# Sparse attention: index queries projected token tile by token tile, the selection of the second query tile begun before the third tile's projection

## The chip, the cores and the metric

The kernel runs on one core of one Trainium2 chip. The metric is the device time of one execution in microseconds (us). TensorE (PE) multiplies, with weight loads shown as an engine of their own (PEld); VectorE (DVE), ScalarE (ACT) and GpSimd (POOL) work on elements; SyncE (SP) starts the transfers between memory and the chip's buffer.

## The reference, cut to what matters

Two decoder layers over 512 tokens of width 1024. Each has a token mixer, a cross attention into 256 memory tokens and a SwiGLU feed-forward network (FFN), and after each of these `x = LayerNorm(alpha * x + y)`. Layer 0 mixes with latent attention, layer 1 with the sparse attention (DSA) that is changed here:

```python
h = x @ w_in            # q 16x64 | k 4x64 | v 4x64 | q_idx 8x64 | k_idx 64 | w_idx 8
...
dots  = einsum('bqhd,bkd->bqhk', q_idx, k_idx) * 64 ** -0.5
score = einsum('bqh,bqhk->bqk', w_idx * 8 ** -0.5, relu(dots))
score = where(causal, score, -inf)
_, sel = top_k(score, 128)           # 128 keys for each query
...                                  # attention over the selected keys, with a bias
```

So for each query of 512 an indexer of eight heads scores all earlier keys; the 128 best keys are kept, and the sixteen heads attend to those alone. Queries of the first token tile (0 to 127) have no more than 128 keys and need no selection.

## The kernel before, in words

Everything is fp32, with each product made of three fast passes: both factors are split into a high and a low part, and `mm3` (L126, L127, L128) adds high x high, high x low and low x high in one PSUM bank. `split` (L102, L104) makes the parts: ACT copies the high part, and DVE (or POOL, if named) subtracts it from the source. `chunk` (L116) loads a piece of weights of up to 128x1024 with SP into `raw`, a ring of three buffers, and splits it into `wh` and `wl`, rings of five. A load waits until the split of the load three places earlier is done with its buffer, and a split until PE is done with the weights five places earlier. PSUM has eight banks, four with the tag "a" and four with "b". `t2` and `t8` are pools of 39 and 9 buffers for intermediate values.

The program is written as one sequence; a scheduler puts it into one fixed order for each engine, and on the chip an engine does its instructions in that order and waits for each one's inputs. So whatever stands behind a waiting instruction on the same engine waits too.

The stages around the change, in the order of the program:

1. *The down-projection of layer 0's FFN* (`out_proj`, n = 0 and then n = 1: the two halves of 512 output columns). For n = 1 it goes over four token tiles of 128 tokens. Behind each tile's products DVE adds the result to x (`residual`, L356), takes statistics (L315), and the tile before is normalised (`Norm.finish`: POOL's L287, DVE's L340, and so on), turned by eight PE transposes (L344) and split for the next stage.
2. *v, index keys and index weights* (loop over token tiles, three chunks of `w_vi`): 24 products of 328 columns for each tile; the keys are copied and transposed (L972), and the four tiles' keys split together.
3. *Index queries and scores*: for each of four pairs of index heads one chunk of `w_qi` is projected for tokens 128 to 511 at once (24 products of 384 columns), split into a stacked form (`stack_q`, DVE's L945 and L946), and scored against the keys for query tiles 1, 2 and 3 (PE's L990 and its neighbour; the relu on ACT, L992; the sum over heads on DVE, L994 for the first head and L996 for the others). Behind the last pair POOL masks the causal triangle of each tile (L999). Tile 1 has 256 keys, tile 2 has 384 and tile 3 has 512.
4. *Selection*: `topk` finds eight maxima of a row (MAX, L1008) and replaces them by a very low number (MATCH_REPLACE, L1009), sixteen such rounds for each of the three tiles, so 48, all on DVE and each dependent on the one before. What was replaced is the selected set, and a last instruction (L1013) makes a mask of it. The rounds are written in between other work: two ahead of each of the two key projections (`w_k`, whose result goes to both halves of the partitions with a subtract on DVE, L1030, and a copy on ACT, L1031), five ahead of each of the eight query projections (`w_q`, low parts of the weights and L953 on POOL), one after each of the next attention items.
5. *Attention*: sixteen items, four query tiles by four groups of heads, each with scores (L1062 to L1064), a softmax (L428, L435, L439, L440), transposes (L1076) with splits (L104, or L107 to L109), the product with v (L1098), and a normalisation (L1100, L1105, L1108, L1109, L1113). The items of tile 0 start inside the query projections.

## Time and profile before

| | |
|---|---|
| median of 3 runs | 1521.48 us (1521.23 to 1521.71) |
| the profiled execution | 1523.14 us, of it 1521.4 us span |
| PE busy | 1490.7 us, 98% of the span |
| DVE busy | 993.9 us, 65% |
| ACT busy | 650.3 us, 43% |
| POOL busy | 305.0 us, 20% |
| granted clock of PE, mean | 0.996 |

A window row of the profile gives the start and end of a stretch, its length, the busy time and the number of instructions of PE, PEld, DVE, ACT and POOL, the granted clock, the busy share of the transfer engines and the rate in GB/s. A timeline row gives start, length, engine, line, operation, output and inputs, and in brackets the idle time before it and what ended that. A group row gives the number of instructions after the x, and behind the bar their busy time in us, the mean of one in ns, and the idle time before them. A row on transfers gives the size of each and the median time from issue to landing in us.

### The profile page before, as it was taken

Reading aid. Unit: us, or ns where it says so; the run is one execution under the profiler, and the core shown is the slowest. Engines: PE = TensorE matmul, PEld = TensorE weight load, DVE = VectorE, ACT = ScalarE, POOL = GpSimd, SP = SyncE. Lnnn points to the kernel's source line nnn. Section 1 sums busy time; section 2 is a strip of 40 time slices with the busy share of each in tenths; the row PEclk is TensorE's granted clock in tenths of the full one; section 3 lists DMA queues with packets and bytes.
Section 4 is the critical chain, followed back from the end, with each engine's and each line's share of the span. In section 5 each row is a group of like instructions: output and inputs, shape, how many; then the busy total and the mean of one; then the engine's idle time right before and its main releaser. Section 6 shows DMA issues by size and latency. Waiting matters only on the chain.

```text
span 1521.4 us, 20233 instructions
## 1 busy us (share of the span) xinstructions
PE 1490.7 (98%) x7642; PEld 1265.9 (83%) x7642; DVE 993.9 (65%) x1739; ACT 650.3 (43%) x1160; POOL 305.0 (20%) x299
## 2 busy tenths in 40 slices
PE   9999999999999999999999989999999999999997
PEld 8788888988898888888898777898889888888886
DVE  7887868554745655654578989675557555666545
ACT  4777753443233333333256588343432433333320
POOL 1322001000032331410024653000002232323002
PEclk9999999999999999999999999999999999999999
DMA  6234424432332233333243146343323233232231
GB/s 216 72 104 114 145 83 131 128 117 70 125 98 92 89 125 98 97 91 104 91 139 104 61 152 224 111 139 97 115 80 125 84 125 97 97 104 78 98 95 56
DMA packets 51143, 166.16 MB, mean 109 GB/s; under 512 B 5284, under 2 KB 11828, under 8 KB 48996
## 3 DMA queue, kind: packets, MB, share of 16 engines
q1 hardware_dynamic: 50468, 163.61, 33.4%
q8 instruction: 60, 0.98, 0.3%
q10 hardware_dynamic: 576, 1.25, 0.2%
q14 instruction: 39, 0.32, 0.1%
HBM read 160.60 MB, written 9.47 MB: 112 GB/s over the span
## 4 chain that ended last, share of the span: by engine, by line
PE 85%; DVE 8%; ACT 2%; issue 2%; DMA 1%; POOL 1%; POOLq 0%; SPq 0%; DVEq 0%; ACTq 0%
PE ps L127 26%; PE ps L126 26%; PE ps L128 26%; DVE t L104 2%; DVE t L1009 2%; DVE m L1008 1%; PE ps L344 1%; ACT t L435 1%; PE ps L1076 1%; DMA t<-scr 1%; ACT t L102 1%; PE ps L660 1%; DVE wl L104 1%; PE ps L786 0%; DVE t L428 0%
## 5 line engine op out<-in xcount | busy, mean ns | idle before, releaser
L126 PE MATMUL ps<-t,wh 128*128 128x512 f32 (+2 forms) x1248 | 451.9, 362 | 6.0 <-DVE t L104 3.4
L127 PE MATMUL ps<-t,wh 128*128 128x512 f32 (+2 forms) x1248 | 450.2, 361 | 1.2 <-DVE t L104 1.2
L128 PE MATMUL ps<-t,wl 128*128 128x512 f32 (+2 forms) x1248 | 450.2, 361 | 0.0
L102 ACT CAST wh<-raw 128x1024 fp32r<-128x1024 f32 (+2 forms) x217 | 226.5, 1044 | 433.5 <-PE ps L127 157.3
L104 DVE TENSOR_TENSOR wl<-raw,wh 128x1024 fp32r<-128x1024 f32 (+2 forms) x196 | 252.6, 1290 | 209.5 <-ACT wh L102 208.5
L126 PE MATMUL ps<-wh,t 128*128 128x512 f32 (+3 forms) x774 | 295.6, 382 | 0.1
L127 PE MATMUL ps<-wl,t 128*128 128x512 f32 (+3 forms) x774 | 293.3, 379 | 0.1
L128 PE MATMUL ps<-wh,t 128*128 128x512 f32 (+3 forms) x774 | 292.9, 378 | 0.0
L126 PEld LDWEIGHTS ps<-t,wh 128*128 128x128 f32 x1248 | 235.5, 189 | 43.2 <-DVE t L104 5.5
L127 PEld LDWEIGHTS ps<-t,wh 128*128 128x128 f32 x1248 | 235.6, 189 | 36.1 <-DVE t L104 1.5
L128 PEld LDWEIGHTS ps<-t,wl 128*128 128x128 f32 x1248 | 235.6, 189 | 35.0
L102 ACT CAST t<-ps 128x512 fp32r<-128x512 f32 (+2 forms) x249 | 122.6, 526 | 129.6 <-PE ps L344 86.5
L126 PEld LDWEIGHTS ps<-wh,t 128*128 128x128 f32 x774 | 146.6, 189 | 25.7 <-ACT t L435 0.4
L128 PEld LDWEIGHTS ps<-wh,t 128*128 128x128 f32 x774 | 146.4, 189 | 25.8
L127 PEld LDWEIGHTS ps<-wl,t 128*128 128x128 f32 x774 | 146.5, 189 | 25.6 <-DVE wl L104 0.5
L287 POOL TENSOR_TENSOR sm<-sm,mhalf 128x1 f32<-128x1 f32 x32 | 30.2, 942 | 682.6 <-DVE sm L285 682.6
L104 DVE TENSOR_TENSOR t<-ps,t 128x512 fp32r<-128x512 f32 (+2 forms) x249 | 143.4, 607 | 19.9 <-ACT t L102 17.6
L102 ACT CAST wh<-t 128x1024 fp32r<-128x1024 f32 x56 | 58.9, 1053 | 141.8 <-PE ps L127 123.6
L104 DVE TENSOR_TENSOR wl<-t,wh 128x1024 fp32r<-128x1024 f32 x56 | 71.3, 1273 | 65.2 <-ACT wh L102 63.2
L889 DVE TENSOR_TENSOR t<-ps,t 128x512 f32<-128x512 f32 x44 | 30.4, 692 | 120.1 <-PE ps L128 120.1
L104 DVE TENSOR_TENSOR t<-t,t 128x512 fp32r<-128x512 f32 (+2 forms) x113 | 84.5, 751 | 27.9 <-ACT t L102 25.7
L102 ACT CAST t<-t 128x512 fp32r<-128x512 f32 (+2 forms) x113 | 64.6, 575 | 56.8 <-POOL t L823 33.6
(179 smaller groups left out, 1645.1 us busy)
## 6 DMA issues: line engine op xcount, KB each, us to landing
raw<-in_ffn_in_dram SPq DMA_DIRECT2D x88, 512.0 KB, 3.5
t<-in_ffn_dg_dram SPq DMA_DIRECT2D x16, 1024.0 KB, 5.1
raw<-in_xa_k_dram SPq DMA_DIRECT2D x16, 512.0 KB, 3.6
raw<-in_xa_v_dram SPq DMA_DIRECT2D x16, 512.0 KB, 3.6
raw<-in_xa_q_dram SPq DMA_DIRECT2D x16, 512.0 KB, 4.3
raw<-in_xa_o_dram SPq DMA_DIRECT2D x16, 512.0 KB, 3.5
raw<-in_ffn_dl_dram SPq DMA_DIRECT2D x12, 512.0 KB, 3.5
scr<-vscr SPq DMA_DIRECT2D x16, 319.5 KB, 4.3
```

What stands on the lines that cost most here:

```text
L102: nc.scalar.copy(h, src)
L104: low[0] = (eng or nc.vector).tensor_tensor(l, src, h.bitcast(F32), op=ALU.subtract)
L126: nc.tensor.matmul(ps, st[0], mv[0], start=start, stop=False, skip_group_check=more)
L127: nc.tensor.matmul(ps, st[0], mv[1], start=False, stop=False, skip_group_check=more)
L128: nc.tensor.matmul(ps, st[1], mv[0], start=False, stop=stop, skip_group_check=more)
L287: nc.gpsimd.tensor_tensor(b, a, mhalf, op=ALU.pow)
L344: nc.tensor.transpose(pt[:, k], x_of(tt)[:, 512 * n + P * k:512 * n + P * k + P], ident)
L435: nc.scalar.activation(Sx, src, AF.Exp, bias=nb, scale=scale, accum_out=self.sm[:, i:i + 1])
L660: nc.tensor.transpose(pt[:, P * qt:P * qt + P], Ss[qt][:, P * kb:P * kb + P], ident)
L889: nc.vector.tensor_tensor(sg, pu, sg, op=ALU.mult)
L1008: nc.vector.max(out=m8, in_=acc[:, :n])
L1009: nc.vector.match_replace(out=acc[:, :n], in_to_replace=m8, in_values=acc[:, :n], imm_value=-3e38)
```

## The change

Four things are done in other ways. First, `w_qi` is laid out by input rows, and its four pieces are loaded and split by `load_wqi`, which the down-projection of layer 0's FFN calls behind its own last weight loads (`mid`). The eight pairs of split pieces (512 columns each) stay in `t2` buffers until the projections are done. Second, index queries are projected for one token tile at a time, with tokens on the output's partitions (`index_q`: 24 products of 512 columns for each of tiles 1, 2 and 3), then copied by ACT, turned back by four PE transposes (`index_turn`) and stacked. Third, scores are made by tile and by half of the heads (`index_scores`, HA the first four and HB the last four), and keys are transposed and split for each tile. Fourth, the order: tile 1's scores are complete before tile 3's index query projection, and selection rounds begin there, four of them ahead of tile 3's turn, two ahead of the first key projection, four more behind tile 3's first scores, two ahead of the second key projection, and then five ahead of each query projection as before.

```diff
...
-    def out_proj(src, w, kc, norm, first, pins=()):
+    def out_proj(src, w, kc, norm, first, pins=(), mid=None):
...
             ws = [weights(n, c) for c in range(kc)] if n else None
+            if n and mid:
+                mid()
...
-    def ffn(i, XT, norm_of, between=None):
+    def ffn(i, XT, norm_of, between=None, mid=None):
...
-        out_proj(lambda k: H[k], lambda n, c: A["ffn_dl"][i, n, c], len(H) // 2, norm, False)
+        out_proj(lambda k: H[k], lambda n, c: A["ffn_dl"][i, n, c], len(H) // 2, norm, False, mid=mid)
...
-    norm = ffn(0, norm.XT, lambda: Norm(load_ln(0, 2), spill=True), general_bias())
+    wqi = []
+
+    def load_wqi():
+        for c in range(4):
+            raw = wp.tile([P, 1024], F32, tag="raw", name=nm("raw"), bufs=3)
+            nc.sync.dma_start(raw, A["w_qi"][c])
+            for i in range(2):
+                wqi.append((t2(FR), t2(FR)))
+                split(*wqi[-1], raw[:, 512 * i:512 * i + 512])
+
+    norm = ffn(0, norm.XT, lambda: Norm(load_ln(0, 2), spill=True), general_bias(), load_wqi)
     r = nc.values_load(flag[0:1, 0:1], engines=(mybir.EngineType.SP,), min_val=0, max_val=1)
     XT = norm.XT
 
...
 
     wvs = [chunk(A["w_vi"][:, NV * k0:NV * k1], (P, k1 - k0, NV)) for k0, k1 in ((0, 3), (3, 6), (6, 8))]
     VD = t8(FR, (P, 4, 4, P))
-    pk = bank("b")
     wi = cp.tile([P, NT, 8], F32, name="wi")
-    for tt in range(NT):
+    KIA, KIB = t2(FR), t2(FR)
+    masks = [None] + [t2() for _ in range(1, NT)]
+
+    def dsa_v(tt):
         pv = bank("a")
-        ts_ = slice(P * tt, P * tt + P)
+        ts_ = ts_of(tt)
         for k in range(NK):
             xh, xl = k_of(XT, k)
             w = wvs[k // 3]
             mm3(pv[:, 0:NV], (xh[:, ts_], xl[:, ts_]), (w[0][:, k % 3], w[1][:, k % 3]), k == 0, k == NK - 1)
+        ki = t2(F32, (P, 2, 64))
+        nc.scalar.copy(ki, pv[:, 264:NV].unsqueeze(1).broadcast_to((P, 2, 64)))
+        nc.vector.tensor_scalar(wi[:, tt], pv[:, 256:264], 8.0 ** -0.5, None, op0=ALU.mult)
+        pk = bank("b", (P, P))
+        nc.tensor.transpose(pk, ki.rearrange("p a b -> p (a b)"), ident)
+        split(KIA[:, ts_], KIB[:, ts_], pk)
         pv4 = pv[:, 0:256].rearrange("p (g d) -> p g d", g=4)
         split(VD[:, tt, :, 0:64], VD[:, tt, :, 64:128], pv4)
-        nc.vector.tensor_scalar(wi[:, tt], pv[:, 256:264], 8.0 ** -0.5, None, op0=ALU.mult)
-        ki = t2(F32, (P, 2, 64))
-        nc.scalar.copy(ki, pv[:, 264:NV].unsqueeze(1).broadcast_to((P, 2, 64)))
-        nc.tensor.transpose(pk[:, ts_], ki.rearrange("p a b -> p (a b)"), ident)
-
-    KIA, KIB = t2(FR), t2(FR)
-    split(KIA, KIB, pk)
-    masks = [None] + [t2() for _ in range(1, NT)]
-    for j in range(4):
-        pq = bank("a")
-        proj(pq, chunk(A["w_qi"][j], (P, NK, P)), XT, (P, S))
+
+    def index_q(qt):
+        ps = bank("a")
+        ts_ = ts_of(qt)
+        for k in range(NK):
+            xh, xl = k_of(XT, k)
+            mm3(ps, (xh[:, ts_], xl[:, ts_]), wqi[k], k == 0, k == NK - 1)
+        qf = t2()
+        nc.scalar.copy(qf, ps)
+        return qf
+
+    def index_turn(qf):
+        pt = bank("a")
+        for j in range(4):
+            nc.tensor.transpose(pt[:, P * j:P * j + P], qf[:, P * j:P * j + P], ident)
         qi = (t2(FR), t2(FR))
-        stack_q(pq[:, P:], qi[0][:, P:], qi[1][:, P:])
-        for qt in range(1, NT):
-            n = P * (qt + 1)
-            ts_ = slice(P * qt, P * qt + P)
-            acc = masks[qt]
-            for e in range(2):
-                h = 2 * j + e
-                ps = bank("b")
-                nc.tensor.matmul(ps[:, :n], qi[e][:, ts_], KIA[:, :n], start=True, stop=False)
-                nc.tensor.matmul(ps[:, :n], qi[e][:, ts_], KIB[:, :n], start=False, stop=True)
-                rl = t2()
-                nc.scalar.activation(rl[:, :n], ps[:, :n], AF.Relu, scale=0.125)
-                if h == 0:
-                    nc.vector.tensor_scalar(acc[:, :n], rl[:, :n], wi[:, qt, 0:1], None, op0=ALU.mult)
-                else:
-                    nc.vector.scalar_tensor_tensor(acc[:, :n], rl[:, :n], wi[:, qt, h:h + 1], acc[:, :n],
-                                                   op0=ALU.mult, op1=ALU.add)
-            if j == 3:
-                nc.gpsimd.affine_select(out=acc[:, n - P:n], in_=acc[:, n - P:n], pattern=[[-1, P]],
-                                        compare_op=ALU.is_ge, fill=-1e30, base=0, channel_multiplier=1)
+        stack_q(pt, qi[0], qi[1])
+        return qi
+
+    def index_scores(qt, qi, heads):
+        n = P * (qt + 1)
+        acc = masks[qt]
+        for h in heads:
+            js = slice(P * (h // 2), P * (h // 2) + P)
+            ps = bank("b")
+            nc.tensor.matmul(ps[:, :n], qi[h % 2][:, js], KIA[:, :n], start=True, stop=False)
+            nc.tensor.matmul(ps[:, :n], qi[h % 2][:, js], KIB[:, :n], start=False, stop=True)
+            rl = t2()
+            nc.scalar.activation(rl[:, :n], ps[:, :n], AF.Relu, scale=0.125)
+            if h == 0:
+                nc.vector.tensor_scalar(acc[:, :n], rl[:, :n], wi[:, qt, 0:1], None, op0=ALU.mult)
+            else:
+                nc.vector.scalar_tensor_tensor(acc[:, :n], rl[:, :n], wi[:, qt, h:h + 1], acc[:, :n],
+                                               op0=ALU.mult, op1=ALU.add)
+        if heads[-1] == 7:
+            nc.gpsimd.affine_select(out=acc[:, n - P:n], in_=acc[:, n - P:n], pattern=[[-1, P]],
+                                    compare_op=ALU.is_ge, fill=-1e30, base=0, channel_multiplier=1)
+
     MK = t8()
 
     def topk(qt, its):
...
 
     todo = [(qt, [i]) for qt in range(1, NT) for i in range(TOPK // 8)]
     NTK, NTI = 5, 1
+
+    def rounds(n):
+        for _ in range(min(n, len(todo))):
+            topk(*todo.pop(0))
+
     KA, KB = [], []
-    for j in range(2):
-        for _ in range(2):
-            topk(*todo.pop(0))
+
+    def k_proj(j):
+        rounds(2)
         (pk,) = proj_tiles([chunk(A["w_k"][j], (P, NK, P), nc.gpsimd)], XT, False)
         kt_ = t8()
         for e in range(2):
...
             nc.scalar.copy(kb[64 - 64 * e:128 - 64 * e], kb[64 * e:64 * e + 64].bitcast(F32))
             KA.append(ka)
             KB.append(kb)
+
+    HA, HB = range(0, 4), range(4, 8)
+    dsa_v(0)
+    dsa_v(1)
+    f1 = index_q(1)
+    dsa_v(2)
+    i1 = index_turn(f1)
+    f2 = index_q(2)
+    index_scores(1, i1, HA)
+    dsa_v(3)
+    index_scores(1, i1, HB)
+    i2 = index_turn(f2)
+    f3 = index_q(3)
+    index_scores(2, i2, HA)
+    rounds(4)
+    i3 = index_turn(f3)
+    k_proj(0)
+    index_scores(2, i2, HB)
+    index_scores(3, i3, HA)
+    rounds(4)
+    k_proj(1)
+    index_scores(3, i3, HB)
+
     def dsa_bias(qt, g):
         n = P * (qt + 1)
         c0 = 127 + 384 - 128 * qt
...
-        for _ in range(min(NTK, len(todo))):
-            topk(*todo.pop(0))
+        rounds(NTK)
...
-        for _ in range(NTI):
-            if todo:
-                topk(*todo.pop(0))
+        rounds(NTI)
...
-    f["w_qi"] = _fm(w[:, 1536:2048])
+    f["w_qi"] = _tm(w[:, 1536:2048], 2, 512)[0]
```

On DVE at the end of layer 0's down-projection (`wl` from `ffn_dl` are raw_10118 and raw_10124, raw_10324 is the first piece of `w_vi`; L356 is the residual add), before:

```order
L104 TENSOR_TENSOR wl_10121<-raw_10118,wh_10120 128x1024
L104 TENSOR_TENSOR t_1386_9996<-t_1382_9988,t_1385_9995 128x512
L104 TENSOR_TENSOR wl_10127<-raw_10124,wh_10126 128x1024
L104 TENSOR_TENSOR wl_10327<-raw_10324,wh_10326 128x984
L356 TENSOR_TENSOR t_658_2508<-t_658_2508,ps_10006 128x512
L356 TENSOR_TENSOR t_658_2508<-t_658_2508,ps_10007 128x512
L315 BN_STATS sm_10101<-t_658_2508 128x6
```

and now, with raw_10130 to raw_10160 the four pieces of `w_qi` and raw_10364 the first of `w_vi`:

```order
L104 TENSOR_TENSOR wl_10121<-raw_10118,wh_10120 128x1024
L104 TENSOR_TENSOR t_1420_10133<-raw_10130,t_1419_10132 128x512
L104 TENSOR_TENSOR t_1422_10137<-raw_10130,t_1421_10136 128x512
L104 TENSOR_TENSOR t_1425_10143<-raw_10140,t_1424_10142 128x512
L104 TENSOR_TENSOR wl_10127<-raw_10124,wh_10126 128x1024
L104 TENSOR_TENSOR t_1427_10147<-raw_10140,t_1426_10146 128x512
L104 TENSOR_TENSOR t_1430_10153<-raw_10150,t_1429_10152 128x512
L104 TENSOR_TENSOR t_1432_10157<-raw_10150,t_1431_10156 128x512
L104 TENSOR_TENSOR t_1435_10163<-raw_10160,t_1434_10162 128x512
L104 TENSOR_TENSOR t_1437_10167<-raw_10160,t_1436_10166 128x512
L104 TENSOR_TENSOR wl_10367<-raw_10364,wh_10366 128x984
L356 TENSOR_TENSOR t_658_2508<-t_658_2508,ps_10006 128x512
```

Between the last split of the down-projection's weights, the first split of `w_vi` and the first residual add there are now eight subtracts of `w_qi`.

On POOL, from the normalisation at the end of that FFN (L287) to the causal masks (L999, now L1024), before, where the five splits are those of two pieces of `w_k` and three of `w_q`:

```order
L287 TENSOR_TENSOR sm_10220<-sm_10218,mhalf 128x1
L287 TENSOR_TENSOR sm_10266<-sm_10264,mhalf 128x1
L287 TENSOR_TENSOR sm_10293<-sm_10291,mhalf 128x1
L104 TENSOR_TENSOR wl_10787<-raw_10784,wh_10786 128x1024
L104 TENSOR_TENSOR wl_10833<-raw_10830,wh_10832 128x1024
L104 TENSOR_TENSOR wl_10891<-raw_10888,wh_10890 128x1024
L104 TENSOR_TENSOR wl_10945<-raw_10942,wh_10944 128x1024
L104 TENSOR_TENSOR wl_11000<-raw_10997,wh_10999 128x1024
L999 AFFINE_SELECT t_1463_10473<-t_1463_10473 128x128
L999 AFFINE_SELECT t_1464_10474<-t_1464_10474 128x128
L999 AFFINE_SELECT t_1465_10475<-t_1465_10475 128x128
L104 TENSOR_TENSOR wl_11056<-raw_11053,wh_11055 128x1024
```

and now:

```order
L287 TENSOR_TENSOR sm_10260<-sm_10258,mhalf 128x1
L287 TENSOR_TENSOR sm_10306<-sm_10304,mhalf 128x1
L104 TENSOR_TENSOR wl_10736<-raw_10733,wh_10735 128x1024
L104 TENSOR_TENSOR wl_10845<-raw_10842,wh_10844 128x1024
L287 TENSOR_TENSOR sm_10333<-sm_10331,mhalf 128x1
L104 TENSOR_TENSOR wl_10931<-raw_10928,wh_10930 128x1024
L104 TENSOR_TENSOR wl_10985<-raw_10982,wh_10984 128x1024
L104 TENSOR_TENSOR wl_11039<-raw_11036,wh_11038 128x1024
L1024 AFFINE_SELECT t_1474_10386<-t_1474_10386 128x128
L104 TENSOR_TENSOR wl_11096<-raw_11093,wh_11095 128x1024
L1024 AFFINE_SELECT t_1475_10387<-t_1475_10387 128x128
L104 TENSOR_TENSOR wl_11176<-raw_11173,wh_11175 128x1024
```

Both `w_k` splits moved ahead of the last tile's L287, and the three masks, which stood together, are each behind a `w_q` split.

On DVE around the first selection round (L1008 and L1009, now L1034 and L1035; L996 and now L1019 and L1021 are the sums over heads; t_1463 and t_1474 are the scores of tile 1), before:

```order
L996 SCALAR_TENSOR_TENSOR t_1463_10473<-t_1527_10735,wi,t_1463_10473 128x256
L996 SCALAR_TENSOR_TENSOR t_1463_10473<-t_1529_10741,wi,t_1463_10473 128x256
L996 SCALAR_TENSOR_TENSOR t_1464_10474<-t_1531_10750,wi,t_1464_10474 128x384
L1008 MAX m_1539_10778<-t_1463_10473 128x8
L996 SCALAR_TENSOR_TENSOR t_1464_10474<-t_1533_10756,wi,t_1464_10474 128x384
L996 SCALAR_TENSOR_TENSOR t_1465_10475<-t_1535_10765,wi,t_1465_10475 128x512
L1009 MATCH_REPLACE t_1463_10473<-m_1539_10778,t_1463_10473 128x256
L996 SCALAR_TENSOR_TENSOR t_1465_10475<-t_1537_10771,wi,t_1465_10475 128x512
L1008 MAX m_1540_10781<-t_1463_10473 128x8
```

and now:

```order
L1021 SCALAR_TENSOR_TENSOR t_1474_10386<-t_1512_10636,wi,t_1474_10386 128x256
L957 TENSOR_TENSOR t_1514_10647<-ps_10642,t_1514_10647 64x512
L958 TENSOR_TENSOR t_1515_10648<-ps_10642,t_1515_10648 64x512
L1034 MAX m_1526_10704<-t_1474_10386 128x8
L1035 MATCH_REPLACE t_1474_10386<-m_1526_10704,t_1474_10386 128x256
L1034 MAX m_1527_10707<-t_1474_10386 128x8
L1035 MATCH_REPLACE t_1474_10386<-m_1527_10707,t_1474_10386 128x256
L1034 MAX m_1528_10710<-t_1474_10386 128x8
L1035 MATCH_REPLACE t_1474_10386<-m_1528_10710,t_1474_10386 128x256
L1034 MAX m_1529_10713<-t_1474_10386 128x8
L1019 TENSOR_SCALAR t_1475_10387<-t_1519_10683,wi 128x384
L1035 MATCH_REPLACE t_1474_10386<-m_1529_10713,t_1474_10386 128x256
```

Before, the first round stands between the last three sums of tiles 2 and 3; now it stands behind tile 1's last sum and tile 2's stacking (L957, L958), and all of the sums of tiles 2 and 3 come behind it, in between rounds.

## The prediction

> **What bounds the kernel now.** I read the page first. It says TensorE (PE), nearly everywhere:
>
> ```profile
> span 1521.4 us, 20233 instructions
> PE 1490.7 (98%) x7642; PEld 1265.9 (83%) x7642; DVE 993.9 (65%) x1739; ACT 650.3 (43%) x1160; POOL 305.0 (20%) x299
> ```
>
> PE is idle for 30.7 us of the span. So I asked next where those are, with the windows around the changed stage (columns: busy us and instructions of PE, PEld, DVE, ACT, POOL; granted clock; DMA share; GB/s):
>
> ```profile
> 750.00:760.00 10.00, 9.99 (x48) 8.03 (x47) 9.73 (x18) 1.18 (x2) 1.39 (x2) 1.00 0.30 105
> 850.00:860.00 10.00, 8.80 (x46) 7.10 (x46) 9.74 (x32) 7.30 (x18) 3.14 (x4) 1.00 0.01 2
> 860.00:870.00 10.00, 7.91 (x37) 6.34 (x38) 9.68 (x26) 4.77 (x11) 5.26 (x8) 1.00 0.01 2
> 870.00:880.00 10.00, 8.14 (x46) 6.83 (x45) 9.66 (x35) 5.08 (x14) 8.24 (x10) 1.00 0.49 157
> 880.00:890.00 10.00, 7.15 (x48) 5.95 (x48) 8.08 (x27) 8.00 (x28) 2.44 (x6) 0.92 0.00 1
> 890.00:900.00 10.00, 10.00 (x54) 9.44 (x53) 7.74 (x30) 7.45 (x23) 6.40 (x9) 0.74 0.54 185
> 900.00:910.00 10.00, 9.60 (x55) 7.52 (x55) 8.86 (x30) 9.41 (x23) 6.52 (x14) 1.00 0.61 210
> 889.00:890.00 1.00, 0.60 (x3) 0.61 (x4) 1.00 (x3) 0.67 (x2) 1.00 (x3) 0.50 0.00 0
> ```
>
> From 850 to 890 PE works 32.0 us of 40: 8.0 us idle, while VectorE (DVE) is 97% busy until 880. There DVE sets the time. Second finding: a granted clock of 0.50 at 889, a mean of 0.92 and 0.74 in the two slices around it. 0.92 means 1.6 us at half, 0.74 means 5.2 us: 6.8 us at half speed, some 3.4 us of work lost. The timeline names the waits in brackets:
>
> ```profile
> 860.43 0.50 PE L126 MATMUL ps<-t,wh 128*128 128x512 f32 x1 [1.29 <-ACT t L952]
> 869.00 0.44 PE L1108 MATMUL ps<-ident,t 128*128 128x128 f32 x2 [1.65 <-POOL t L440]
> 878.36 0.35 PE L1063 MATMUL ps<-t,t 128*128 128x256 f32 x1 [1.59 <-DVE sm L428]
> 886.63 0.63 PE L1076 MATMUL ps<-ident,t 128*128 128x128 f32 x4 [1.89 <-DVE t L1105]
> 888.16 0.62 PE L1098 MATMUL ps<-t,t 128*128 128x512 f32 x1 [0.34 <-ACT t L109]
> 889.40 0.69 PE L1108 MATMUL ps<-ident,t 128*128 128x128 f32 x2 [0.61 <-POOL t L440]
> 813.29 0.43 DVE L1008 MAX8 m<-t 128x8 f32<-128x256 f32 x1 [0.19 <-POOL t L999]
> 813.64 1.26 DVE L996 SCALAR_TENSOR_TENSOR t<-t,wi,t 128x384 f32<-128x384 f32 x2
> 814.82 0.08 DVE L1009 MATCH_VALUE_LOAD t<-m,t 128x8 f32 x1
> 885.64 0.84 DVE L1105 TENSOR_TENSOR t<-ps,t 64x256 f32<-64x256 f32 x2
> ```
>
> The last three waits before 889.4 add up to 2.84 us and lie among transposes; behind them PE starts at half clock. DVE's queue runs from the first selection round (813.29) to the operation that releases PE (885.64): 72.35 us. When this queue ends decides when PE runs free again.
>
> **The change, part by part.**
>
> *Tail of layer 0's FFN.* Four w_qi loads and eight splits now stand ahead of the first w_vi split, and that ahead of the first residual add, on DVE and in the raw ring of three.
>
> ```profile
> 737.29 1.05 ACT L102 CAST wh<-raw 128x1024 fp32r<-128x1024 f32 x1 [4.10 <-issue]
> 738.38 1.23 DVE L104 TENSOR_TENSOR wl<-raw,wh 128x1024 fp32r<-128x1024 f32 x1 [3.84 <-ACT wh L102]
> 743.78 1.18 DVE L104 TENSOR_TENSOR wl<-raw,wh 128x984 fp32r<-128x984 f32 x1 [4.18 <-ACT wh L102]
> 746.09 1.37 DVE L356 TENSOR_TENSOR t<-t,ps 128x512 f32<-128x512 f32 x2 [1.12 <-PE ps L128]
> L104 DVE TENSOR_TENSOR t<-raw,t 128x512 fp32r<-128x512 f32 x4 | 2.6, 684 | 0.0
> raw<-in_ffn_dl_dram SPq DMA_DIRECT2D x6, 512.0 KB, 3.5
> raw<-in_w_q_dram SPq DMA_DIRECT2D x2, 512.0 KB, 4.8
> ```
>
> Of the eight subtracts (0.68 each), three fit into the idle 3.84 us ahead of the last down-projection split, which ended at 739.6 and now ends near 740.4. That frees the slot for the third w_qi load (740.4); the fourth (740.8) and the first w_vi load (741.1, once the second load's last subtract is done) go right behind on SP's queue. A load alone takes 3.5 us, two close together 4.8; three I estimate at a little over 5: w_vi is there at 746.3, its cast (1.05) and subtract (1.18) end at 748.6. The residual add, at 746.09 now, waits for that: **+2.5**. Bounds: w_vi in 3.5 us gives 746.9, +0.8; the three one after another at 3.5 each give 753.2, +7.1. I take 2.5, by the nearest row (4.8). It is not hidden: those adds free PE's banks for the token projections, and DVE's share of 0.97 from 750 to 760 shows no slack to catch up in.
>
> *PE's own work.*
>
> ```profile
> 783.08 0.31 PE L126 MATMUL ps<-wh,t 128*128 128x328 f32 x1
> 783.52 0.34 PE L126 MATMUL ps<-t,wh 128*128 128x384 f32 x1
> ...
> 784.57 0.33 PE L126 MATMUL ps<-t,wh 128*128 128x384 f32 x1
> 829.37 0.39 PE L126 MATMUL ps<-t,wh 128*128 128x512 f32 x1
> 830.05 0.39 PE L126 MATMUL ps<-t,wh 128*128 128x512 f32 x1
> 249.18 0.87 PE ps L344 x8
> ```
>
> Three products lie between neighbouring L126 rows (784.57 is the second after 783.52); the last row is the chain's, eight transposes in 0.87. Index projections: 96 of 384 columns at 0.175 (1.05 for six) = 16.8; now 72 of 512 at 0.227 (0.68 for three) = 16.3. Twelve transposes more at 0.109 = 1.3. Net **+0.8** on PE, hidden while DVE bounds.
>
> *First selection round.* Now the four v projections end at 783.5. The first third of the fourth ends five k-steps of 0.44 earlier, 781.3; in the new order two index projections (10.9), one turn (0.4), four scores of 256 columns (eight products, about 1.0 by 0.147 for 328 columns) and the 2.5 above come first: 796.1. That third's weight slots are what the first w_q chunk waits for, and in POOL's order three w_q splits now stand ahead of tile 1's causal select:
>
> ```profile
> 829.60 2.41 POOL L104 TENSOR_TENSOR wl<-raw,wh 128x1024 fp32r<-128x1024 f32 x1 [2.12 <-ACT wh L102]
> L999 POOL TENSOR_SCALAR_AFFINE_SELECT t<-t 128x128 f32<-128x128 f32 x3 | 1.7, 572 | 3.2 <-DVE t L996 3.2
> ```
>
> Cast 1.05, three splits of 2.41 with starts between them, select 0.57: the first round starts near **805.3** instead of 813.29. Without these splits ahead it would be 2.5 earlier, since the last scores of tile 1 end by 801.
>
> Two more edits I cost at nothing. On POOL two w_k splits now stand ahead of the last tile's L287, the power that its normalisation needs; their cover is the time until that tile's statistics are there, by my walk some 1.2 us more than the splits need. If it is gone, one split (2.41) lands on tile 3's projections and on the first round. On SP's queue the four w_qi loads leave the place behind w_vi, so that w_k and w_q come sooner; PE waits for neither there, so nothing is gained, and a delay of one load (3.5) would be hidden behind the two index projections.
>
> *DVE's queue from there.* It loses the three sums behind 813.29 (1.26 + 0.75) and gains sixteen sums of tiles 2 and 3, a stacking pair for tile 3, and the last mask, which stood behind 885.64:
>
> ```profile
> L996 DVE SCALAR_TENSOR_TENSOR t<-t,wi,t 128x512 f32<-128x512 f32 x7 | 5.2, 748 | 0.3
> L996 DVE SCALAR_TENSOR_TENSOR t<-t,wi,t 128x384 f32<-128x384 f32 x7 | 4.3, 617 | 0.3
> L1030 DVE TENSOR_TENSOR t<-ps,t 64x512 fp32r<-64x512 f32 x4 | 2.8, 689 | 0.1
> L1013 DVE TENSOR_SCALAR t<-t 128x512 fp32r<-128x512 f32 x1 | 0.4, 427 | 0.0
> ```
>
> The sums are L996's, each tile's first one (a plain multiply) taken at the same price; the pair is priced by L1030, a subtract of the same shape, and the mask is L1013.
>
> 72.35 − 2.0 + 8 × 0.617 + 8 × 0.748 + 2 × 0.689 + 0.43 = 83.1. Against that, sums between a round's MAX and its MATCH_REPLACE overlap both: 0.43 + 1.26 took 1.53 (813.29 to 814.82), 0.16 saved. In DVE's order 16 fewer neighbours belong to one chain of rounds: 16 × 0.16 = 2.6 saved (half that if only one edge overlaps). 80.5 us: the queue ends at 885.8, **+0.2**, between −2.3 (tail +0.8, select 0.8 sooner) and +4.8 (tail +7.1). So the early start is eaten by the longer queue.
>
> PE arrives at the queue's end later: 2.5 + 0.8, and I estimate 1.8 for a new stall at 818 to 821. There tile 3's scores need a bank whose relu stands on ACT behind a key copy, which waits for a DVE subtract behind the rounds. A wait of this kind is there now:
>
> ```profile
> 819.54 0.62 ACT L1031 CAST t<-t 64x512 fp32r<-64x512 f32 x1 [1.63 <-DVE t L1030]
> ```
>
> These 5.1 us replace idle time: of the 8.0 us some 3 stay, and the free run starts where the queue lets it, 0.2 later.
>
> *The clock.* The waits of 1.89, 0.34 and 0.61 us shrink, PE being later, and the emptied stretch before 889 with them. I take **−2.5** of the 3.4 us, and 0 and −3.4 as bounds: DVE and ACT stay busy to 0.89 and 0.94 at 900 to 910, so some PE time regained there will be lost to waits.
>
> The Trainium skill, "TensorE: Matmul & The Clock Gate", section "What's actually happening", has a free-running window of 3413 ns and half rate after an idle one, and "Part 4: PE-mode transpose" adds that transposes do not count as busy in the same way. Read by gaps alone (its section "Why this matters for your kernels" allows gaps up to some 3 us) the 1.89 us here would have cost no clock; the trace disagrees, unless the transposes among the waits count as idle. By that stricter reading the clock term would be 0 for me as well, the time of the first rival.
>
> Sum: +0.2 − 2.5 = −2.3. The profiled execution took 1523.14 us, 1.7 above its span and 1.7 above the median of 1521.48; it would become 1520.8, the median **1519.2**.
>
> **Rivals.** *1. The clock falls anyway* (chance 0.22). The new stall at 818, or the 3 us of waits that remain after 855, empty a window as the old one did. For it: summed waits of only 2.8 us did it once. Against: the same waits at 860 to 879, each 1.3 to 1.65 us, did not. Time: 1521.48 + 0.2 = 1521.7.
>
> *2. The tail is cheap* (0.20). w_vi lands in 3.5 us, first round at 803.6, queue end 884.1 (−1.5), the whole clock loss gone (−3.4): 1516.6; with the select ahead of one split less, 2.4 less, 1514.2. For it: DMA share is only 0.30 at 750 to 760. Against: three loads start within 0.7 us.
>
> *3. Slower* (0.17). The three loads land one behind the other at 3.5 us each, the residual adds come 7.1 later and everything behind them 4.6 later than forecast: first round 809.9, queue end 890.4, +4.8, and PE meets the same waits with the same half clock. Time 1521.48 + 4.8 = 1526.3. It decides from 3.0 us on, that is when w_vi lands more than 8 us after its issue at the same clock loss. For it: nothing on SP's queue orders w_vi ahead. Against: 4.8 us for two.
>
> **How the numbers follow.** The forecast has 0.38, 0.03 is left over. Its own range is 1517 to 1521.2: clock −3.4 to −1, queue −1 to +0.7. About 0.2% (3.0 us) is what a measurement of this kernel can tell from no change: 1518.4 to 1524.5 is "same". Faster: rival 2 with 0.19 and some 0.4 of the forecast, 0.36 in all. Slower: rival 3 with 0.15, some of rival 1 with a longer tail, 0.22. Same: 0.42. For eight in ten I go from 1514.8, nearly rival 2's far end, to 1525.8, most of rival 3.
>
> **What would show it.** The residual add at 748.6 (below 747: rival 2; above 750: rival 3). The first MAX at 805.3. The three POOL splits ahead of tile 1's select. DVE busy 0.95 or more from there to about 886. PE idle of 3 us instead of 8 from 850 to 890, and no slice with clock 0.50 between 880 and 900; a half clock elsewhere says rival 1. The forecast is wrong if the free run starts more than 2 us from 889.6, or if PE stalls in a place not named here, above all between 796 and 821, where the new order puts ACT copies and splits behind each other.

## The result: 1533.7 us, slower by 0.8%

| | before | after |
|---|---|---|
| median | 1521.6 us (1521.2 to 1521.9, 4 runs) | 1533.7 us (1533.0 to 1535.9, 4 runs) |
| ratio, 95% interval | | 1.0082 (1.0065 to 1.0099) |
| profiled execution, span | 1523.1, 1521.4 us | 1534.0, 1532.2 us |

I had forecast 1519.2 and a range up to 1525.8. One execution in all that follows, of kernel 9 below, took 8403.9 us and is left out of its median. Profiled executions of kernels that are alike up to the changed stage reach it at times up to 2.8 us apart, so I measure the stage by itself: from SP's first load for the down-projection (`ffn_dl`) to its fifth load for layer 1's cross-attention values (`xa_v`). Timelines of before and, below, of after:

```profile
698.79 24.63 SPq L116 DMA_DIRECT2D raw<-in_ffn_dl_dram  x6
1038.59 12.50 SPq L116 DMA_DIRECT2D raw<-in_xa_v_dram  x4
```

```profile
698.22 24.63 SPq L116 DMA_DIRECT2D raw<-in_ffn_dl_dram  x6
1049.39 5.76 SPq L116 DMA_DIRECT2D raw<-in_xa_v_dram  x2
```

339.8 us became 351.2, +11.4: all of the loss is here. The windows of after (columns as in the prediction) show where PE lost it:

```profile
740.00:750.00 10.00, 9.37 (x42) 7.42 (x41) 6.75 (x11) 4.17 (x6) 0.00 (x0) 1.00 0.72 232
770.00:780.00 10.00, 6.98 (x32) 6.66 (x33) 8.05 (x11) 1.81 (x4) 4.50 (x3) 0.66 0.47 158
810.00:820.00 10.00, 8.51 (x42) 6.80 (x41) 9.53 (x25) 3.74 (x8) 0.29 (x1) 1.00 0.18 54
820.00:830.00 10.00, 7.29 (x33) 5.57 (x32) 9.60 (x27) 7.38 (x15) 2.87 (x2) 1.00 0.15 52
890.00:900.00 10.00, 8.46 (x51) 7.63 (x51) 5.48 (x29) 7.91 (x29) 1.93 (x4) 0.83 0.08 27
900.00:910.00 10.00, 9.45 (x53) 8.60 (x54) 7.98 (x30) 8.02 (x25) 8.00 (x12) 0.83 0.49 182
```

From 700 to 950 PE is idle for 16.8 us; before it was 9.5. And there are now two stretches at half clock, one at 770 to 780 (0.66: 6.8 us at half, 3.4 lost) and the old one (0.83 twice, 3.4 lost). 7.2 of idle time, 3.4 of clock and the 0.8 forecast for added products and transposes make up the 11.4. The timeline of after names two pairs of rows that I had not looked for:

```profile
768.45 5.26 POOL L104 TENSOR_TENSOR wl<-raw,wh 128x1024 fp32r<-128x1024 f32 x2
768.65 5.61 DVE L340 SCALAR_TENSOR_TENSOR t<-t,sm,t 128x512 f32<-128x512 f32 x2
771.56 1.12 PE L344 MATMUL ps<-ident,t 128*128 128x128 f32 x4 [2.14 <-DVE t L340]
774.41 1.09 PE L344 MATMUL ps<-ident,t 128*128 128x128 f32 x4 [1.46 <-DVE t L340]
805.41 5.58 DVE L1021 SCALAR_TENSOR_TENSOR t<-t,wi,t 128x256 f32<-128x256 f32 x4
812.46 0.43 DVE L1034 MAX8 m<-t 128x8 f32<-128x256 f32 x1
827.82 0.50 PE L1014 MATMUL ps<-t,t 128*128 128x512 f32 x1 [2.37 <-ACT t L1017]
```

The same work before, tile 2's L340 and the group of the sums of 256 columns:

```profile
767.39 1.41 DVE L340 SCALAR_TENSOR_TENSOR t<-t,sm,t 128x512 f32<-128x512 f32 x2
L996 DVE SCALAR_TENSOR_TENSOR t<-t,wi,t 128x256 f32<-128x256 f32 x7 | 3.4, 485 | 2.1 <-ACT t L992 2.1
```

Tile 2's two L340, 1.41 us together for any other tile, took 5.61 while POOL made the low parts of w_k. Tile 1's last four sums, 0.485 us each before, took 5.58 while POOL made those of w_q (three of them from 802.23). PE waited 2.14 us, fell to half clock at 771.4 and waited another 1.46; the first round came at 812.46, only 0.8 sooner than before. I read this as DVE being held by POOL. That reading, and what the rest is worth, had to be tested.

### The profile page after: what moved, and what is told of

Its sections match the earlier page's. It is cut to its first block, busy times and chain, and to the rows that moved or that the text cites. A ratio compares the mean times of both kernels' runs of the same rounds, so it can differ in the third digit from the quotient of the medians.

```text
span 1532.2 us, 20237 instructions
## 1 busy us (share of the span) xinstructions
PE 1494.5 (98%) x7630; PEld 1266.0 (83%) x7630; DVE 1002.1 (65%) x1744; ACT 651.5 (43%) x1168; POOL 304.6 (20%) x299
## 4 chain that ended last, share of the span: by engine, by line
PE 84%; DVE 10%; ACT 3%; issue 2%; DMA 1%; POOL 0%; POOLq 0%; SPq 0%; DVEq 0%; ACTq 0%
PE ps L127 26%; PE ps L126 26%; PE ps L128 26%; DVE t L1035 2%; DVE t L104 2%; DVE m L1034 1%; ACT t L437 1%; PE ps L344 1%; DMA t<-scr 1%; ACT t L102 1%; DVE t L1021 1%; PE ps L1130 1%; DVE wl L104 1%; PE ps L662 1%; ACT wh L102 1%
## 5 line engine op out<-in xcount | busy, mean ns | idle before, releaser
L126 PE MATMUL ps<-t,wh 128*128 128x512 f32 (+1 forms) x1216 | 441.3, 363 | 5.9 <-DVE t L104 3.4
L127 PE MATMUL ps<-t,wh 128*128 128x512 f32 (+1 forms) x1216 | 439.5, 362 | 1.2 <-DVE t L104 1.2
L128 PE MATMUL ps<-t,wl 128*128 128x512 f32 (+1 forms) x1216 | 439.4, 361 | 0.0
L102 ACT CAST wh<-raw 128x1024 fp32r<-128x1024 f32 (+2 forms) x213 | 222.2, 1044 | 424.7 <-PE ps L127 157.3
L104 DVE TENSOR_TENSOR wl<-raw,wh 128x1024 fp32r<-128x1024 f32 (+2 forms) x192 | 247.5, 1290 | 200.1 <-ACT wh L102 198.9
L126 PEld LDWEIGHTS ps<-t,wh 128*128 128x128 f32 x1216 | 229.5, 189 | 43.3 <-DVE t L104 5.5
L127 PEld LDWEIGHTS ps<-t,wh 128*128 128x128 f32 x1216 | 229.6, 189 | 35.7 <-DVE t L104 1.5
L128 PEld LDWEIGHTS ps<-t,wl 128*128 128x128 f32 x1216 | 229.5, 189 | 34.9
L287 POOL TENSOR_TENSOR sm<-sm,mhalf 128x1 f32<-128x1 f32 x32 | 30.1, 942 | 683.4 <-DVE sm L285 683.4
```

The lines of the kernel that those rows point to most:

```text
L102: nc.scalar.copy(h, src)
L104: low[0] = (eng or nc.vector).tensor_tensor(l, src, h.bitcast(F32), op=ALU.subtract)
L126: nc.tensor.matmul(ps, st[0], mv[0], start=start, stop=False, skip_group_check=more)
L127: nc.tensor.matmul(ps, st[0], mv[1], start=False, stop=False, skip_group_check=more)
L128: nc.tensor.matmul(ps, st[1], mv[0], start=False, stop=stop, skip_group_check=more)
L287: nc.gpsimd.tensor_tensor(b, a, mhalf, op=ALU.pow)
```

## The experiments

All comparisons are with the kernel before on the same chip, whose median in these sets was 1520.8 to 1521.6. The stage is that of the one profiled execution. The last column splits it further: PE's idle time in it, and what was lost to the clock (half of the time at a granted clock of 0.50).

| kernel | median | ratio (95%) | stage | idle / clock |
|---|---|---|---|---|
| before | | 1 | 339.8 | 9.7 / 3.4 |
| the change | 1533.7 | 1.0082 (1.0065 to 1.0099) | 351.2 | 16.9 / 6.8 |
| 1. w_k low parts on DVE | 1528.0 | 1.0048 (1.0031 to 1.0064) | 345.5 | 13.8 / 3.4 |
| 2. w_q low parts behind the select | 1532.6 | 1.0075 (1.0058 to 1.0091) | 351.5 | 16.3 / 8.5 |
| 3. 1 and 2 | 1526.3 | 1.0031 (1.0019 to 1.0044) | 343.6 | 11.0 / 5.1 |
| 4. the change, short POOL splits | 1526.6 | 1.0031 (1.0018 to 1.0043) | 346.9 | 14.4 / 5.1 |
| 5. the change, key copies on POOL | 1530.6 | 1.0063 (1.0045 to 1.0080) | 348.4 | 17.1 / 3.4 |
| 6. 3 and key copies on POOL | 1524.8 | 1.0031 (1.0018 to 1.0043) | 342.6 | 12.9 / 1.7 |
| 7. 3 without the early rounds | 1526.3 | 1.0027 (1.0017 to 1.0037) | 344.0 | 11.9 / 5.1 |
| 8. 6 and short splits ("all mends") | 1520.7 | 0.9995 (0.9986 to 1.0005) | 339.8 | 11.4 / 0 |
| 9. before, short splits | 1519.2 | 0.9979 (0.9969 to 0.9989) | 337.6 | 8.8 / 1.7 |
| 10. 8, tile 1's scores ahead of q of tile 2 | 1521.1 | 0.9995 (0.9985 to 1.0005) | 341.9 | 10.5 / 1.7 |
| 11. 8, tile 1's scores ahead of the fourth v | 1520.9 | 0.9997 (0.9987 to 1.0006) | 339.3 | 10.4 / 0 |
| 12. 8, w_qi loads behind w_vi | 1520.3 | 0.9992 (0.9983 to 1.0002) | 338.9 | 10.0 / 1.7 |
| 13. 9, half of the rounds | 1516.3 | 0.9966 (0.9952 to 0.9980) | 333.3 | 5.9 / 0 |
| 14. 8, half of the rounds | 1515.3 | 0.9967 (0.9953 to 0.9981) | 336.0 | 8.2 / 0 |

The clock differs between executions of one kernel too: of kernel 6's eight, two had a mean granted clock of 0.993 and took 1528.7 and 1528.8 us, six had 0.995 to 0.999 and took 1523.8 to 1525.7. So a clock term of 1.7 or 3.4 us in one profiled execution is not yet a property of the kernel.

### Does POOL hold DVE? (1 to 4)

Kernel 1 puts the low parts of w_k on DVE, behind the last split of the normalisation (`done`):

```diff
     XT = norm.XT
+    done = low[0]
-        (pk,) = proj_tiles([chunk(A["w_k"][j], (P, NK, P), nc.gpsimd)], XT, False)
+        (pk,) = proj_tiles([chunk(A["w_k"][j], (P, NK, P), None, (None, done))], XT, False)
```

> The two low-part subtracts of w_k are on DVE, behind the last split of the FFN's last normalisation, and POOL has none until w_q. Theory A (a DVE instruction with two operands in SBUF stands still while POOL's subtract runs): the second L340 of tile 2, 2.83 us with the change, is back at 0.72 to 0.75, as is the first; PE's waits of 2.14 and 1.46 us at 771 to 775 go, and with them the half clock of 770 to 780 (mean 0.66, 3.4 us lost): 5 to 7 us less, 1527 to 1529. Tile 1's last sums still meet POOL's w_q splits and stay near 1.4 us each. Theory B (the new order itself is late: w_vi behind w_qi, and the stalls at 811 to 828; the long L340 only fills time in which PE would wait anyway): first MAX still after 811, time 1532 to 1534. Theory C (the length of L340 is a wait for POOL's power, L287, counted as busy): L340 stays near 2.8 us.

Groups of lines from 740 to 910, kernel 1:

```profile
L340 DVE SCALAR_TENSOR_TENSOR t<-t,sm,t 128x512 f32<-128x512 f32 x8 | 5.6, 744 | 0.0
L1022 DVE SCALAR_TENSOR_TENSOR t<-t,wi,t 128x256 f32<-128x256 f32 x7 | 6.7, 960 | 1.0 <-ACT t L1018 0.5
```

All eight L340 have a mean of 744 ns again (with the change 1270). The clock is 1.00 up to 820, and the stage is 5.7 us shorter, the time 1528.0, as A had it. L287 stayed on POOL, so C falls. Tile 1's sums still have a mean of 960: nothing was done for them.

Kernel 2 puts the w_q low parts of the first three chunks behind tile 1's select (`sel[1]` is its instruction):

```diff
-            nc.gpsimd.affine_select(...)
+            sel[qt] = nc.gpsimd.affine_select(...)
...
-        (pq,) = proj_tiles([chunk(A["w_q"][j], (P, NK, P), nc.gpsimd)], XT, False)
+        (pq,) = proj_tiles([chunk(A["w_q"][j], (P, NK, P), nc.gpsimd, (None, sel[1] if j < 3 else None))], XT, False)
```

> The low parts of the first three w_q chunks stand on POOL behind tile 1's causal select, the w_k ones stay where the change has them. Theory A: tile 1's last four sums take 0.48 to 0.5 us each in place of 1.4 (4 in 1.95 instead of 5.58), the first MAX is near 808.8 instead of 812.5, PE's wait of 1.29 us at 811.8 goes; tile 2's sums may meet the splits in turn, up to 2.4 us for each that does: 1530 to 1533. The tile 2 L340 stays at 2.8 and the half clock of 770 to 780 stays. Theory B: the first MAX sooner by the POOL queue alone (one select, under 1 us), 1533 to 1534.

Groups of kernel 2:

```profile
L340 DVE SCALAR_TENSOR_TENSOR t<-t,sm,t 128x512 f32<-128x512 f32 x8 | 9.8, 1270 | 0.0
L1023 DVE SCALAR_TENSOR_TENSOR t<-t,wi,t 128x256 f32<-128x256 f32 x7 | 3.4, 484 | 1.0 <-DVE t L1023 0.5
L1023 DVE SCALAR_TENSOR_TENSOR t<-t,wi,t 128x384 f32<-128x384 f32 x7 | 5.9, 850 | 0.0
```

Tile 1's sums are back at 484 ns, the first MAX came at 807.7. But tile 2's now meet the splits (850 in place of 605), and the stage is as long as with the change: a meeting moved is not a meeting saved.

> Both edits: w_k low parts on DVE behind the normalisation, first three w_q low parts on POOL behind tile 1's select. Theory A: first MAX at 801 to 803, no half clock before 880, 1522 to 1526, so the whole loss of the change or most of it is gone; what the prediction had forecast (1519) is possible if the second half clock goes too. Theory B: no better than 1531.

Kernel 3, with both edits, has its first MAX at 802.73, ten us sooner than the change, and 7.5 us less stage; the time, 1526.3, is just above A's range, and a half clock that A had excluded is there (0.83 at 820 to 830). Most of what is left ahead of 850 lies at 810 to 830:

```profile
817.68 0.62 ACT L1065 CAST t<-t 64x512 fp32r<-64x512 f32 x1 [2.96 <-DVE t L1064]
820.05 0.79 PE L1017 MATMUL ps<-t,t 128*128 128x512 f32 x1 [3.02 <-ACT t L1020]
```

In kernel 4 the order is that of the change, and each POOL subtract of 1024 columns is cut into four of 256:

```diff
-            low[0] = (eng or nc.vector).tensor_tensor(l, src, h.bitcast(F32), op=ALU.subtract)
+            if eng is nc.gpsimd and l.shape[-1] == 1024:
+                for c in range(0, 1024, 256):
+                    sl = slice(c, c + 256)
+                    low[0] = eng.tensor_tensor(l[:, sl], src[:, sl], h[:, sl].bitcast(F32), op=ALU.subtract)
+            else:
+                low[0] = (eng or nc.vector).tensor_tensor(l, src, h.bitcast(F32), op=ALU.subtract)
```

> The order of the change, but each POOL low-part subtract of 1024 columns is cut into four of 256. The work is the same, one meeting can last only a quarter as long. Theory A: the two L340 of tile 2 take 1.4 to 2.7 us together instead of 3.5, none over 1.4; tile 1's last four sums 2 to 4.5 us instead of 5.58; PE's gaps at 771 to 775 under 1.5 us and the half clock there may go: 1525 to 1532. Theory C, and any theory that has DVE wait for POOL's results: no change, 1533 to 1536 (POOL's work gets a little longer).

```profile
L345 DVE SCALAR_TENSOR_TENSOR t<-t,sm,t 128x512 f32<-128x512 f32 x8 | 6.6, 866 | 0.4 <-POOL sm L292 0.4
L1026 DVE SCALAR_TENSOR_TENSOR t<-t,wi,t 128x256 f32<-128x256 f32 x7 | 4.4, 629 | 1.0 <-DVE t L1026 0.5
```

(L345 is L340 here.) Same work, same order, a quarter of the length: L340's excess falls from 4.2 us (9.8 − 5.6) to 1.0, the sums' from 3.3 to 1.0 (L343, L338 here, is now held too: 6.2 us in place of 5.6). PE's waits at the normalisation fall to 0.51, 0.42 and 1.17, without a half clock there; one follows a wait of 3.54 us at 820.5, the place of kernel 3's. So it is POOL's running instruction that DVE waits for, and what it costs goes by the length of that instruction.

### What else is lost (5 to 8, 12)

The row of kernel 3 above is the stall that the prediction had named: on ACT a copy of the keys' low part waits for DVE's subtract behind selection rounds, and the relus behind it hold PE's bank. Kernels 5 and 6 give that copy to POOL:

```diff
-            nc.scalar.copy(kb[64 - 64 * e:128 - 64 * e], kb[64 * e:64 * e + 64].bitcast(F32))
+            nc.gpsimd.tensor_copy(kb[64 - 64 * e:128 - 64 * e], kb[64 * e:64 * e + 64].bitcast(F32))
```

> The change as it is, with only the four key copies moved from ACT to POOL. L340 and tile 1's sums stay slow (2.8 and 1.4 us), the half clock at 770 to 780 stays. PE's wait of 2.37 us at 827.8 goes. Theory P: 2 to 3 us less, 1531 to 1532. Theory Q: the queue's end stays, 1533 to 1534.

> As the run with both edits (w_k low parts on DVE, three w_q low parts behind tile 1's select: 1526.3), and the four copies of the keys' low parts between partition halves go from ACT to POOL. There ACT stood 2.96 us at 815 waiting for the keys' subtract, which DVE had behind selection rounds; the relus of the index scores stood behind it, PE waited 3.02 us at 820 and ran at half clock in 820 to 830 (mean 0.83, some 1.7 us lost). Theory P (this stall and the clock are what is left of the loss): the wait falls under 1 us, no half clock at 820 to 830, 4 to 5 us less: 1521 to 1523. Theory Q (DVE's queue sets the end, so PE only comes to wait later): the gap moves to 855 to 890, gain 0 to 2 us: 1524.5 to 1526.5.

Kernel 5 has 2.8 us less stage, about what P had, but not by P's mechanism: the wait that should have gone is still there, since ACT's next cast of the keys waits for the same subtract.

```profile
823.66 0.58 ACT L1058 CAST t<-ps 64x512 fp32r<-64x512 f32 x1 [2.26 <-DVE t L1061]
825.40 0.50 PE L1014 MATMUL ps<-t,t 128*128 128x512 f32 x1 [2.16 <-ACT t L1017]
```

PE's idle time in the stage is 0.2 us longer than with the change; the gain is 3.4 us less lost to the clock (the half clock of 890 to 905 is gone, and the mean granted clock is 0.996 to 0.998 in its four executions, 0.993 to 0.995 in those of the change; why is open). On kernel 3 the copy brings 1.0: PE's wait is 2.82 in place of 3.02, and 1524.8 lies in Q's range. So with the copy gone ACT waits for the same subtract behind the rounds with its next cast.

Kernel 7 takes the two calls `rounds(4)` out of kernel 3:

> As the run with both edits, without the two groups of four early rounds: two rounds ahead of each key projection and five ahead of each query projection as before the change, the last four behind attention items. Theory P: the keys' subtract has only two rounds ahead of it, ACT's wait and PE's wait near 815 to 820 fall under 1.5 us and the half clock there goes; 1521 to 1524. Theory Q: DVE stands idle before 812 for want of rounds, the queue starts with tile 2's and tile 3's sums and ends no sooner: 1525 to 1529.

Its first MAX came at 803.9 all the same, since the rounds ahead of the first key projection stand nearly there; the half clock at 820 to 830 stayed (0.66). In the order on DVE the keys' subtract still has nine whole rounds ahead of it, so the edit did not do what P needed: it is inconclusive on P. It does show that writing the early rounds in is worth nothing to kernel 3 (1526.3 both).

> The run with key copies on POOL and each POOL low-part subtract of 1024 columns cut into four of 256. DVE's meetings with POOL (sums of tiles 2 and 3, 2.2 us over their undisturbed time, the masks 1.5) get shorter: 1 to 3 us less than with the key copies alone under Q, since all of that lies in DVE's queue; 0 to 1 less under P.

Kernel 8 (6 with the cut of 4) is at 0.9995: the loss is gone, in the stage to 0.1 us, though by another sum: PE is idle 1.7 us longer than before, and the 3.4 us of clock are not lost. 4.1 us of the median came with the cut, more than expected; of the 5.2 us between the two profiled executions 2.8 lie in the stage and 2.6 ahead of it. In eight kernels with whole splits the first down-projection load stands at 696.6 to 699.4 us, in eight with short ones at 694.2 to 696.0.

Kernel 12 undoes the load inside the down-projection: `load_wqi()` stands behind the w_vi loads.

> As the run with all three mends, but the four w_qi loads and their splits stand behind the w_vi loads, no longer inside the down-projection. The first residual add comes on time again (PE's waits of 0.4 and 0.5 us at the n = 1 tiles, 0.9 to 1.2 in sister runs, go). But the eight subtracts (5.5 us) then lie among the normalisations, where DVE is 97% busy. If that stretch has no slack, as the prediction has it: PE waits for L340's successors, 2 to 5 us longer, 1522 to 1526. If the loads' place ahead of w_vi is what costs: 1 to 2 us faster, 1518.5 to 1520.

Neither: 1520.3, in the stage 1.0 us less, in the median 0.4, which is within the intervals. PE's wait of 0.42 us at the residual add is gone, the one at L345 grew from 0.54 to 0.79. So DVE had more slack among the normalisations than its busy share of 0.97 had made me think.

### Does the end of DVE's queue set the time? (9 to 11, 13, 14)

Kernel 9, the control, is the kernel before with only the cut:

> The kernel before the change, with each POOL low-part subtract of 1024 columns cut into four of 256. It tells how much of the gain of short splits belongs to the change. If DVE and POOL meet only with the change: the stage from the first down-projection load to layer 1's FFN is as long as before (339.8 us), the whole kernel 0 to 2 us faster by meetings elsewhere. If short splits are better in any order, for another reason (a shorter way from weights to PE, say): the stage gets 2 us or more shorter.

2.2 us less stage, where I had set the border to another reason than meetings; and the traces do not show meetings as the reason. In the kernel before, every sum and every L340 of the stage keeps its length, and only tile 1's mask is clearly held (0.86 us at 834.04); in kernel 9 that mask takes 1.29, and three sums are held as well (0.72 in place of 0.48). Its 2.2 us are 0.9 of idle time and 1.7 of clock, less 0.4 of other time; why short splits do that stays open. Its median is 1.5 us below that of kernel 8, and it has no part of the change in it. Against it, the change with all mends is 2.2 us longer in the stage.

Kernels 10 and 11 let rounds start sooner still. Kernel 11 puts `index_scores(1, i1, HB)` ahead of `dsa_v(3)`; kernel 10 uses this order (of the lines that it moves only the new places are shown):

```diff
     dsa_v(2)
     i1 = index_turn(f1)
+    dsa_v(3)
+    index_scores(1, i1, HA)
+    index_scores(1, i1, HB)
     f2 = index_q(2)
+    rounds(4)
+    f3 = index_q(3)
+    i2 = index_turn(f2)
+    rounds(4)
+    index_scores(2, i2, HA)
+    i3 = index_turn(f3)
+    k_proj(0)
...
```

> The kernel of the run with all three mends (w_k low parts on DVE, short POOL splits, three w_q low parts behind the select, key copies on POOL: 1520.7), with another order: all eight heads' scores of tile 1 stand behind the third and fourth v projection and ahead of tile 2's index query projection (5.4 us of products), with rounds from there. First MAX near 794 in place of 799. Theory Q (DVE's queue sets the end, so what counts is how early it starts and that it has no holes): PE's idle time of 850 to 890 shrinks from 6.5 us to 1 to 3 us, 3 to 5.5 us less: 1515 to 1518. Theory P (PE's stalls in the stage set it): no gain over 1 us, or slower by new stalls: 1520 to 1523.

> As the run with all three mends, but only the second half of tile 1's scores goes ahead of the fourth v projection (3.6 us of products): first MAX near 795.7 in place of 799. Theory Q: 2 to 3.6 us less, 1517 to 1519. Theory P: 1520 to 1522.

The last MAX of all selections, in before, in kernel 8 and in kernel 11:

```profile
884.24 0.69 DVE L1008 MAX8 m<-t 128x8 f32<-128x512 f32 x1
```

```profile
874.59 0.69 DVE L1042 MAX8 m<-t 128x8 f32<-128x512 f32 x1
```

```profile
872.31 0.70 DVE L1042 MAX8 m<-t 128x8 f32<-128x512 f32 x1
```

Counted from the first down-projection load (698.8, 694.5, 695.2), the rounds end at 185.4, 180.1 and 177.1: 5 and 8 us sooner than before. The stage is the same to 0.5 us, and of PE's idle time between 140 and 205 us behind that load (8.4 us before) 7.1 and 8.2 are left. In kernel 10 the rounds end at 176.2 and the stage is 2.1 us longer, 1.7 of it by the clock. Q falls: the end of the rounds is not what PE waits for. The last two kernels take the queue away: eight rounds for each tile in place of sixteen (half as many keys are selected).

```diff
-        if its[-1] < TOPK // 8 - 1:
+        if its[-1] < TOPK // 16 - 1:
...
-    todo = [(qt, [i]) for qt in range(1, NT) for i in range(TOPK // 8)]
+    todo = [(qt, [i]) for qt in range(1, NT) for i in range(TOPK // 16)]
```

> The kernel before the change with short POOL splits, with eight selection rounds for each tile in place of sixteen (24 of 48 left out, so half as many keys are kept). This takes some 27 to 30 us out of DVE's queue. Theory Q (the end of the queue of rounds sets when PE runs free): the rounds end before 855, PE's idle time from 850 to 890 (6.9 us) falls under 2 us and the half clock behind it goes: 6 to 9 us less, 1510 to 1513. Theory R (PE's waits there are the attention items' own chains over ACT, POOL and DVE, whatever DVE's queue is behind them): 4 to 6 us of idle time stay, 0 to 3 us less, 1516 to 1519.

> The change with all three mends, with eight selection rounds for each tile in place of sixteen (half as many keys are kept). Theory Q: as for the kernel before with half of the rounds, 1510 to 1514. Theory R: 4 to 6 us of PE's idle time of 850 to 890 stay, 1517 to 1520.

Windows of kernel 13:

```profile
850.00:860.00 10.00, 8.98 (x45) 7.42 (x44) 1.97 (x8) 5.57 (x14) 4.80 (x9) 1.00 0.01 2
860.00:870.00 10.00, 10.00 (x57) 8.57 (x55) 3.07 (x15) 4.84 (x12) 7.38 (x12) 1.00 0.24 69
870.00:880.00 10.00, 7.38 (x52) 6.18 (x50) 4.47 (x25) 8.50 (x30) 3.01 (x6) 1.00 0.25 89
880.00:890.00 10.00, 9.19 (x55) 7.17 (x54) 8.52 (x32) 8.02 (x25) 8.53 (x17) 1.00 0.53 184
```

and its longest wait in the timeline:

```profile
878.19 0.63 PE L1081 MATMUL ps<-ident,t 128*128 128x128 f32 x4 [1.27 <-DVE t L1110]
```

The rounds end at 842, DVE is idle for 20 of the 30 us behind 850, and PE still stands idle for 4.5 us (6.9 in kernel 9; 4.5 against 6.4 in 14 and 8). The waits are steps of the attention items: 1.27 us for L1110 (L1105 before), 1.02 and less for ACT's and POOL's parts. Leaving 24 rounds out brought 4.3 and 3.9 us of stage; 2.9 and 3.2 of it are idle time, and 1.7 of kernel 13's are the clock. Theory R is right on the idle time; by the medians kernel 13 lies in R's range and kernel 14 between R and Q. So some 3 us of PE's idle time in the stage are bound to the amount of DVE's work, and nothing measurable to the moment at which it starts.

## Why the prediction was wrong, step by step

**The tail: nearly right.** The residual add was forecast 2.5 us late. Counted from the first load it went from 47.3 to 49.2, +1.9; PE waited 0.63 us at the n = 1 tiles and 0.51 at the first L344. That it is not hidden was too strong: kernel 12 puts it at 1 us of the stage at most.

**"Two more edits I cost at nothing": the step that failed.** I priced the w_k splits ahead of L287 by the delay of L287, POOL's own queue. L287 was not delayed by them. The splits held DVE's L340 of the tile before, an instruction that needs nothing from these splits: what it does need of POOL, its own tile's L287, was done at 768.48. Price: 5.7 us of stage (kernel 1), of it up to 3.4 by the clock. The same is true of the three w_q splits: their 2.41 each were in my sum as a delay of the select, not as a hold on the four sums ahead of it. So 805.3 became 812.46. Counted from the first load, the first MAX was forecast at 106.5 and came at 114.2 with the change and, with both groups of splits out of the way, at 104.4 (kernel 3).

The Trainium skill has the rule: in "SBUF — State Buffer", section "SBUF: two separate sides", DVE and GpSimd share one pair of SBUF ports under an exclusive lock, taken by whichever starts first, for the whole instruction; a DVE instruction takes part if it has two inputs in SBUF (against a GpSimd instruction that reads SBUF) or runs in a mode with two ports. The trace agrees: L340 and the sums have two tensors in SBUF, POOL's splits read SBUF, and each of the two L340 took 2.8 us in place of 0.74, while the two splits took 5.26 together in place of 4.8. I had read the orders of DVE and of POOL each for itself. Laid side by side with the times they would have shown it: no L340 or L996 lies inside a POOL split in the trace of before.

**The new stall at 818 to 821: right, a little small.** Forecast 1.8; measured 2.37 at 827.8, and ACT's key copy did wait 2.29 us for DVE's subtract at 825.45. But the copy is only the first to wait there: without it PE still waited 2.16 (kernel 5).

**The length of DVE's queue: mis-sized.** I had it 8.2 us longer (80.5 for 72.35). From the first MAX to the last it took 70.95 us before, 74.46 with the change and 75.27 in kernel 8, so it grew by some 4. Why by no more is open.

**"When this queue ends decides when PE runs free again": wrong.** The saturated DVE beside PE's idle time was the whole argument. With the meetings mended the rounds ended 5 us sooner, and most of PE's waits stayed. So even with the failed step mended no gain was found (kernel 8, 0.9995).

**The clock: half right.** The half clock is gone in kernel 8 (all slices of the stage 1.00), but the change as it stands kept it, in two pieces, at 890 to 905 and got a second one. One of the three waits that I had summed for it was not part of its cause: 0.92 in 880 to 890 puts the fall at 888.4, ahead of the wait that ended at 889.4.

**The rivals.** The third had the right sign by another mechanism (loads one behind the other), which did not happen: the first w_vi split came in time. The first had a clock that falls anyway, which came true at 890 to 905, but not its time. None was near 1533.

## What to carry to other kernels

When a change moves work of POOL in time, look at what DVE does in those microseconds, above all at instructions with two operands in SBUF; the price of a meeting goes by the length of POOL's instruction, so cut long ones. A saturated engine beside an idle one is not yet its cause: take half of its work away and see whether the idle time goes. Measure a stage between two of its own loads when what lies ahead of it varies by as much as the effect, and look at idle time and clock apart: kernel 5 gained what was expected of it by the clock alone, with the wait that it was to remove still there.
